# Hybrid decoder layer on one core: gate rows of the second half of the tokens taken from two forms of x that q and k use

## The chip, the core and the metric

One core of a Trainium2 chip runs the whole program. The time is device microseconds of one execution; the median of the runs counts. The engines that matter here are TensorE (PE, with its weight loads PEld), VectorE (DVE), ScalarE (ACT), GpSimd (POOL) and SyncE (SP), which issues most of the DMAs. Each engine takes its instructions in the order in which they stand in its own list and waits on semaphores where an operand or a buffer isn't ready.

## What is computed

One decoder layer on x of 1024 tokens by 1024 channels in float32: rms norm, gated linear attention (GLA), residual; rms norm, a squared-ReLU MLP with 4096 hidden units, residual; final rms norm. What bears on the change is the input projection and the gates:

```python
proj = h @ w_in                          # h = rms_norm(x) * g_mix
q, k, v, r, gk_low = split(proj)         # 512, 512, 1024, 1024 and 16 columns
log_a = log_sigmoid(gk_low @ w_gk_up + b_gk) / 16
b = cumsum(log_a)                        # per chunk; decays are exp(b), exp(-b)
```

q and k are multiplied by decays from `log_a`, and then the tokens go through the attention chunk by chunk.

## The kernel before

**Products.** Each float32 operand is split into a high part (ScalarE, line 81, a copy rounded to fp32r) and a low part (VectorE, line 82, the difference), and a product is three matmuls: high by high, high by low, low by high. A projection is made by a seven-product scheme of 2 by 2 blocks: block names "11", "12", "21", "22" mean half of the channels and half of the tokens (for x) or of the columns (for a weight), and the seven operands are such blocks or sums of them. A step is one of the seven products: 48 matmuls of 512 columns in four lanes (128 rows of output each) and two halves of the channels. Operands of a step are made one step ahead, from tiles `big` (8 buffers, four for a step).

**Order.** q and k together are one projection with steps Q0 to Q6, which take the products in the order 0, 5, 1, 2, 3, 4, 6; then v has V0 to V6, and r has R0 to R4 (two of its products are done later). After that come eight chunks of the attention, the output projection, and the MLP. In the profiled run Q0 begins at 6.5 us, Q1 at 21.4, Q2 at 32.6, Q5 at 65.9, V0 at 87.7, R0 at 169.6, the chunks at 220, the output projection at 299; PE's last matmul ends at 985.6. PE's list is written by hand: it follows the program's text, with functions hung in between by `hooks` (keys are projection, step, and for some a lane and a quarter of the channels). The lists of the other engines are made by a scheduler from the program's priorities and from an `order_after` here and there, which puts one instruction behind another in the list.

**x in forms.** In Q the x blocks come in as `vx` tiles, get scaled by g_mix (line 366 on ScalarE, line 388 on GpSimd) and are combined: step Q1 uses block 21, Q2 uses 12 - 11, Q4 uses 22, and Q5 uses 22 - 12. Each pair of split operands is kept in HBM (`keep`, line 360) for v and r.

**Evacuations.** A product ends in four PSUM banks: tags `gl` (5 banks) and `mm` (3 banks). `qk_into` (from line 475) copies the first product's banks to `hq` on ScalarE (line 485) and adds the later ones on VectorE (line 481).

**Gates.** `wgs` holds w_gk split into high and low parts, laid out so that one 128-column weight load serves both (`split_gate`, line 436, 4 ScalarE and 4 VectorE instructions). The 16 gate columns need 16 matmuls for each half of the tokens ("gate rows", in a bank `mm`). The first half's run between Q0 and Q1 (`gk_first`), from the operands of products 0 and 5, and ScalarE copies them out (line 831). The second half's need blocks 12 and 22 of x: `x12_load` brings block 12 again, `x12_split` scales and splits it in V4, and `gk_second` runs 8 matmuls ahead of V5 and 8 near its end. `token_rms` squares the token rows for the rms; `spread_rms` (line 525) turns four rms columns into a 128 by 512 tile: VectorE writes 8 diagonals (line 534), PE multiplies them by ones (two matmuls), ScalarE copies the bank (line 538), VectorE multiplies the gate rows by it (line 543), and the product is split (lines 544 and 545). `gate_in` multiplies by w_gk_up, and `prep_fast` makes decays per head and multiplies q and k by them (from line 572).

Of the kernel before, what the change touches and what calls it, by code (L numbers as in the profile page):

```python
# [48 lines left out]
def hybrid_trunk(ctx: ExitStack, tc: tile.TileContext, x, xT, w_head, w_r, w_gk, w_up,  # L49
# [10 lines left out]
    def new(tag, dtype=F32):  # L60
        count[0] += 1
        pool_ = ps if tag in ("mm", "gl") else sb
        return pool_.tile(SHAPE.get(tag, [P, 1024]), dtype, tag=tag, bufs=BUFS[tag], name=f"{tag}{count[0]}")

    def f32(ap):
        return ap.bitcast(F32)

    def mm(o, w, m, start, stop, partial=False):

        pe.matmul(o, w, m, start=start, stop=stop, skip_group_check=partial)  # L70
# [50 lines left out]
    def run(general):  # L121
# [312 lines left out]
        wgs5 = wgs.rearrange("p (k g b r) -> p k g b r", k=8, g=4, b=2)  # L434
        wus = new("wup", F32R)

        def split_gate():
# [8 lines left out]

        box = {}

        def gk_rows(pg, kts, part, start, stop):

            for kt in kts:
                for hl in range(2):
                    mm(pg, wgs[:, kt * P:(kt + 1) * P], part(kt, hl), start and kt == kts[0] and hl == 0,
                       stop and kt == kts[-1] and hl == 1)
            return pg

        def token_rms(ts):
            for t in ts:
# [18 lines left out]
        def qk_into(n, lane, p_):  # L477
            d = qk_view(int(PART[n][0]) - 1, lane)[:, half(int(PART[n][1]) - 1)]
            with tc.high_priority():
                if n in (3, 4, 5):  # L480
                    op = dve.tensor_tensor(d, p_, d, op=ALU.add)
                    if n == 5 and lane:
                        order_after(tc, op, last["s1" if lane == 1 else "s1_low"], wait=False)
                else:
                    op = act.activation(d, p_, AF.Copy)
                    if n == 0:
                        order_after(tc, op, last["split"], wait=False)

        v = {}

# [34 lines left out]
        def spread_rms(hf):  # L525

            u, st = new("g4", F32R), new("st", F32R)
            rh, rl, r = st[:, 0:4], st[:, 4:8], rstd1[:, hf * 4:hf * 4 + 4]
            dve.tensor_copy(rh, r)
            dve.tensor_tensor(rl, r, f32(rh), op=ALU.subtract)  # L530
            pb = new("mm")
            for l, part_ in enumerate((rh, rl)):
                for c in range(4):
                    dve.tensor_scalar(u[:, l * 512 + c * P:l * 512 + c * P + P], ident, f32(part_)[:, c:c + 1], None, op0=ALU.mult)
                mm(pb, ones_r, u[:, half(l)], l == 0, l == 1)
            w_ = new("g4")
            dg, rbc = w_[:, 512:1024], w_[:, 0:512]
            act.activation(rbc, pb, AF.Copy)
            if hf == 0:
                box["gk"] = new("g4", F32R)  # L540
            raw, gk = box["raw"][hf], box["gk"][:, half(hf)]
            dst = raw if hf == 0 else dg
            dve.tensor_tensor(dst, raw, rbc, op=ALU.mult)
            act.activation(gk, dst, AF.Copy)
            dve.tensor_tensor(gk[64:128, :], dst[64:128, :], f32(gk[64:128, :]), op=ALU.subtract)


        def chunks(ap):
# [262 lines left out]
        xlive = {}  # L811
        xq_split = xq.split

        xq.first = lambda n, kh: scale_x(kh, *{5: ("21",), 1: ("11", "12"), 2: ("22",)}.get(n, ()))

        def remember(n):
            xlive[n] = xq_split(n)
# [2 lines left out]
        xlive[0] = ops_a[0][1]  # L820

        xk, xr_ = KeptX((0, 5)), KeptX()

        def gk_first():
            pg = gk_rows(new("mm"), range(KT), lambda kt, hl: xlive[0 if kt < 4 else 5][kt % 4 // 2][:, kt % 2, hl, :], True, True)
            box["raw"] = [pg]

        def gk_first_out():
            u, pg = new("g4"), box["raw"][0]
            box["raw"] = [u[:, 0:512]]  # L830
            act.activation(u[:, 0:512], pg, AF.Copy)  # L831

        def x12_load():
            box["x12"] = [new("raw"), new("g4")]
            for kh in range(2):
                nc.sync.dma_start(box["x12"][kh].rearrange("p (k t) -> p k t", k=2), x_piece(2 * kh, 2, 1))

        def x12_split():
            for kh in range(2):
                raw, hi, lo = box["x12"][kh], new("g4", F32R), new("g4" if kh else "raw", F32R)  # L840
                for k in range(2):
                    scaled_split(hi[:, half(k)], lo[:, half(k)], raw[:, half(k)], 2 * kh + k)
                box["x12"][kh] = hi, lo

        def gk_second(part):
            if part == 0:
                box["raw"].append(gk_rows(new("mm"), range(4, KT), lambda kt, hl: xk.tiles[3][kt % 4 // 2][:, kt % 2, hl, :], True, False))
            else:
                gk_rows(box["raw"][1], range(4), lambda kt, hl: box["x12"][kt // 2][hl][:, half(kt % 2)], False, True)

        wv = weight_side(True, from_v, dve, late=True)
        wR = weight_side(True, from_r, dve, late="r")
# [10 lines left out]
        hooks = {(0, 1): (gk_first,), (0, 1, "then"): (gk_first_out,), (0, 3): (split_up,),  # L863
                 (0, 4): (g(token_rms, range(0, 4)),), (0, 5): (g(token_rms, range(4, 8)),),
                 (1, 0, 0, 3): (g(spread_rms, 0),),
                 (2, 4): (r_last,),
                 (1, 2): (x12_load,), (1, 4): (x12_split,), (1, 5): (g(gk_second, 0),),
                 (1, 5, 3, 3): (g(gk_second, 1),), (1, 6, 0, 1): (g(spread_rms, 1),)}
        if not general:
            hooks.update({(1, 0, 2, 3): (g(gate_in, 0, 0, "mm"), g(gate_in, 1, 0, "mm")),  # L870
                          (1, 0, 3, 3): (g(gate_in, 2, 0, "mm"),),
                          (1, 1, 0, 1): (g(gate_in, 3, 0, "mm"), g(prep_fast, 0, 0)),
                          (1, 2): (x12_load,),
                          (1, 2, "then"): (g(prep_fast, 1, 0),), (1, 3, "then"): (g(prep_fast, 2, 0),),
                          (1, 4): (), (1, 4, "then"): (g(prep_fast, 3, 0), x12_split),
                          (1, 5): (g(gk_second, 0),),
                          (1, 6, 3, 1): (g(gate_in, 0, 1, "mm"), g(prep_fast, 0, 1)),
                          (2, 0, 0, 0): (g(gate_in, 1, 1, "mm"), g(prep_fast, 1, 1)),
                          (2, 0, 0, 2): (g(gate_in, 2, 1, "mm"),), (2, 0, 1, 0): (g(gate_in, 3, 1, "mm"),),
                          (2, 0, 3, 3): (g(prep_fast, 2, 1),), (2, 3, "then"): (g(prep_fast, 3, 1),),  # L880
                          (2, 4, 2, 1): (g(operands, 0, "mm"),)})
        chunks_of([(wqk, xq, 0, qk_into, PLAIN), (xk, wv, 1, v_into, PLAIN), (xr_, wR, 1, r_into, R_FIRST)], ops_a, hooks, {},
                  turns={(0, 1): ("X", split_gate, "W"), (0, 2): ("x", "X", "w", "W", lambda: last.update(sums=last["split"], s1=last["sum"], s1_low=last["low"]), "n"),
                         (0, 3): ("W", "x", "X", "n"), (2, 3): ("x", "X", "W", g(wR.sums, 3))})

        last_v = box["v"]
# [7 lines left out]
        if not general:  # L894
            v_split(1)
        for c in range(TT):
            if c == 4 and not general:

                over = new("st")
                dve.tensor_reduce(over[:, 0:1], top, axis=mybir.AxisListType.X, op=ALU.max)  # L900
                dve.tensor_scalar(over[:, 1:2], over[:, 0:1], RANGE, None, op0=ALU.is_gt)
                pf = new("gl")
                mm(pf[:, 0:1], ones, over[:, 1:2], True, True)
                dve.tensor_copy(flag, pf[:, 0:1])
            more = c + 1 < TT
            if general:
                if c % 4 == 0:
                    for h in range(H):
                        prep_general(h, c // 4)
                operands(c)  # L910
                if c:
                    v_split(c)
            elif more:
                operands(c + 1, "mm")
                if c:
                    v_split(c + 1)
            if more:
                if c or general:
                    load_xt(*R_PARTS[c + 1])
                if c in (2, 4):  # L920
                    load_r(5 + c // 2)
            r_part(*R_PARTS[c])
            outputs(c)
            if more:
                new_state(c)
            if c:
                outputs_T(c - 1)
# [312 lines left out]
```

## Time and profile before

| | |
|---|---|
| median of 3 runs | 996.23 us (995.94 to 997.4) |
| profiled execution | 996.73 us, its span 995.0 us |
| granted TensorE clock, mean | 0.997 |
| instructions in the span | 12256 |
| moved by DMA | 193.65 MB, mean 195 GB/s |
| PE waiting for others, whole span | 1.8 us in three waits |
| DMA share of Q3, Q4, Q5, Q6 | 0.84, 0.93, 0.95, 1.05 |

Tile names in the profile leave numbers out: `g` is a tile of tag g4 (gate rows, token rows and others), `mm` and `gl` are PSUM banks, `wa` and `wb` weights, `raw` sums of x. In a row of the timeline stand start, length, engine, line, operation, out<-in, shape, count, and in brackets the idle time before it with what ended it. Line numbers are those of the kernel that the row belongs to.

### The profile page before, as it was taken

Reading aid. Unit: us, or ns where it says so; the run is one execution under the profiler, and the core shown is the slowest. Engines: PE = TensorE matmul, PEld = TensorE weight load, DVE = VectorE, ACT = ScalarE, POOL = GpSimd, SP = SyncE. Lnnn points to the kernel's source line nnn. Section 1 sums busy time; section 2 is a strip of 40 time slices with the busy share of each in tenths; the row PEclk is TensorE's granted clock in tenths of the full one; section 3 lists DMA queues with packets and bytes.
Section 4 is the critical chain, followed back from the end, with each engine's and each line's share of the span. In section 5 each row is a group of like instructions: output and inputs, shape, how many; then the busy total and the mean of one; then the engine's idle time right before and its main releaser. Section 6 shows DMA issues by size and latency. Waiting matters only on the chain.

```text
span 995.0 us, 12256 instructions
## 1 busy us (share of the span) xinstructions
PE 983.5 (99%) x4508; PEld 820.4 (82%) x4508; DVE 748.7 (75%) x912; ACT 564.1 (57%) x860; POOL 237.0 (24%) x146
## 2 busy tenths in 40 slices
PE   9999999999999999999999999999999999999996
PEld 7788888889988888888888888888888888888885
DVE  5996796768899999699662359974339966569976
ACT  7785564887894376666524446332447433566455
POOL 3000010213440000224042142233133224242270
PEclk9999999999999999999999999999999999999998
DMA  9899786575373257651225993367683225971004
GB/s 271 313 319 380 282 295 215 212 242 196 118 280 108 85 196 312 254 221 33 84 99 206 298 303 89 83 175 260 223 324 100 65 63 212 365 283 49 1 1 173
DMA packets 135693, 193.65 MB, mean 195 GB/s; under 512 B 39240, under 2 KB 100808, under 8 KB 124104
## 3 DMA queue, kind: packets, MB, share of 16 engines
q1 hardware_dynamic: 135064, 192.37, 56.0%
q8 instruction: 37, 0.61, 0.3%
q10 hardware_dynamic: 560, 0.40, 0.1%
q14 instruction: 32, 0.26, 0.1%
HBM read 146.62 MB, written 46.14 MB: 194 GB/s over the span
## 4 chain that ended last, share of the span: by engine, by line
PE 92%; DMA 2%; DVE 2%; ACT 2%; SPq 1%; issue 1%; DVEq 0%; ACTq 0%
PE gl L70 61%; PE mm L70 30%; DMA wb<-in_w_head 1%; DMA wa<-in_w_head 1%; DVE vx L1096 0%; PE mm L657 0%; DVE big L82 0%; ACT g L717 0%; PE mm L736 0%; ACT wb L81 0%; SPq L337 0%; DVE big L804 0%; PE gl L736 0%; DVE g L1137 0%; DVE g L726 0%
## 5 line engine op out<-in xcount | busy, mean ns | idle before, releaser
L70 PE MATMUL gl<-big,big 128*128 128x512 f32 x2700 | 626.4, 389 | 0.7 <-DVE big L82 0.4
L70 PEld LDWEIGHTS gl<-big,big 128*128 128x128 f32 x2700 | 506.5, 188 | 106.5 <-DVE big L82 1.1
L70 PE MATMUL mm<-big,big 128*128 128x512 f32 (+1 forms) x1248 | 291.7, 387 | 0.0
L70 PEld LDWEIGHTS mm<-big,big 128*128 128x128 f32 x1248 | 232.7, 188 | 48.2 <-ACT g L831 0.5
L82 DVE TENSOR_TENSOR big<-wa,big 128x1024 fp32r<-128x1024 f32 (+1 forms) x118 | 155.2, 1335 | 85.6 <-ACT big L81 84.6
L81 ACT ACTIVATE big<-wa 128x1024 fp32r<-128x1024 f32 (+1 forms) x118 | 119.2, 1039 | 127.5 <-PE gl L70 67.0
L186 POOL TENSOR_TENSOR wa<-wa,wb 128x1024 f32<-128x1024 f32 x14 | 42.0, 3011 | 299.9 <-DVE big L82 205.9
L186 POOL TENSOR_TENSOR wa<-wa,wa 128x1024 f32<-128x1024 f32 x28 | 80.0, 2866 | 132.8 <-DVE big L82 132.1
L82 DVE TENSOR_TENSOR big<-wb,big 128x1024 fp32r<-128x1024 f32 x50 | 64.4, 1305 | 27.8 <-ACT big L81 27.8
L81 ACT ACTIVATE big<-wb 128x1024 fp32r<-128x1024 f32 x50 | 51.1, 1054 | 56.8 <-PE gl L70 26.6
L82 DVE TENSOR_TENSOR big<-hq,big 128x1024 fp32r<-128x1024 f32 x48 | 61.5, 1290 | 26.7 <-ACT big L81 26.6
L82 DVE TENSOR_TENSOR big<-raw,big 128x1024 fp32r<-128x1024 f32 x42 | 67.6, 1630 | 4.9 <-ACT big L81 4.9
L81 ACT ACTIVATE big<-hq 128x1024 fp32r<-128x1024 f32 x48 | 48.7, 1052 | 39.4 <-PE gl L70 19.5
L81 ACT ACTIVATE big<-raw 128x1024 fp32r<-128x1024 f32 x42 | 43.4, 1055 | 37.9 <-DVE raw L186 17.8
L186 POOL TENSOR_TENSOR wa<-wb,wa 128x1024 f32<-128x1024 f32 x14 | 41.1, 2947 | 39.7 <-DVE big L82 39.7
L577 POOL COPY top<-g 128x4 f32<-128x4 f32 x8 | 10.1, 1267 | 167.8 <-DVE g L569 167.8
L1030 ACT ACTIVATE hq<-hq 128x1024 f32<-128x1024 f32 x24 | 25.3, 1056 | 40.9 <-DVE hq L1023 40.9
L699 POOL TENSOR_SCALAR g<-g,est 128x256 f32<-128x256 f32 x28 | 29.2, 1059 | 52.2 <-DVE g L696 33.3
L1021 ACT ACTIVATE hq<-gl 128x512 f32<-128x512 f32 x36 | 21.4, 593 | 30.6 <-PE gl L70 30.6
L70 PE MATMUL gl<-wb,wa 128*128 128x256 f32 x180 | 32.1, 310 | 0.0
L1023 DVE TENSOR_TENSOR hq<-gl,hq 128x512 f32<-128x512 f32 x24 | 16.0, 685 | 19.8 <-PE gl L70 19.8
L1068 DVE TENSOR_TENSOR vx<-gl,vx 128x512 f32<-128x512 f32 x44 | 29.1, 679 | 0.9 <-PE gl L70 0.8
(206 smaller groups left out, 898.7 us busy)
## 6 DMA issues: line engine op xcount, KB each, us to landing
big<-xw SPq DMA_DIRECT2D x42, 1024.0 KB, 6.9
big<-xv SPq DMA_DIRECT2D x20, 1024.0 KB, 6.4
xv<-big SPq DMA_DIRECT2D x14, 1024.0 KB, 8.5
xw<-big SPq DMA_DIRECT2D x14, 1024.0 KB, 4.3
wa<-in_w_ff SPq DMA_DIRECT2D x32, 256.0 KB, 4.0
wb<-in_w_ff SPq DMA_DIRECT2D x32, 256.0 KB, 3.9
wa<-in_w_ff SPq DMA_DIRECT2D x16, 512.0 KB, 6.6
wb<-in_w_ff SPq DMA_DIRECT2D x16, 512.0 KB, 5.5
```

The lines of the kernel that those rows point to most:

```text
L70: pe.matmul(o, w, m, start=start, stop=stop, skip_group_check=partial)
L81: last["split"] = act.activation(hi, src, AF.Copy)
L82: last["low"] = dve.tensor_tensor(lo, src, f32(hi), op=ALU.subtract)
L186: op = self.eng.tensor_tensor(*(self.ap(b, kp, 2) for b in (o, x_, y_)), op=op)
L577: pool.tensor_copy(top[:, 8 * h + 4 * hf:8 * h + 4 * hf + 4].unsqueeze(2), a[:, :, P - 1:P])
L699: pool.tensor_scalar(S[:, vs], Z[:, vs], g, None, op0=ALU.mult)
L1021: act.activation(d, p_, AF.Copy)
L1023: dve.tensor_tensor(d, p_, d, op=ALU.add)
L1030: act.activation(d2, d2, AF.Relu)
L1068: dve.tensor_tensor(yd, p_, yd, op=ALU.add)
```

## The change

The second half's gate rows are taken from the operands of Q4 (22) and Q5 (22 - 12). Since x12 W1 + x22 W2 = x22 (W1 + W2) - (x22 - x12) W1, new gate weights W1 + W2 and -W1 are formed and split (`split_gate_again`), and the 16 matmuls run between Q4 and Q5. The loading, scaling and splitting of block 12 in V goes. `spread_rms(1)` moves from V6 to V0, one lane behind `spread_rms(0)`; the first heads' decays move about one step up, and those of the second half from V6 to R3 into V5 to R0. ScalarE's first four evacuations (product 0) are put behind the scalings and splits of Q2's x, and the copy of the first gate bank goes in between the scalings. The range check's two VectorE instructions move from chunk 4 to chunk 2. The diff, cut:

```diff
+        def split_gate_again():
+            t = wgu[:, 128:256]
+            for op in (dve.tensor_tensor(t[:, 0:64], wgr[:, 0:64], wgr[:, 64:128], op=ALU.add),
+                       dve.tensor_scalar(t[:, 64:128], wgr[:, 0:64], -1.0, None, op0=ALU.mult)):
+                order_after(tc, op, last["low"], wait=False)
+            box["wgs"] = new("g4", F32R)
+            split_gate(box["wgs"], t.rearrange("p (k r) -> p k r", r=16))
...
+        def gk_rows(wgs, forms):
+
+            box["pg"] = new("mm")
+            for kt in range(KT):
                 for hl in range(2):
+                    mm(box["pg"], wgs[:, kt * P:(kt + 1) * P], forms[kt // 4][kt % 4 // 2][:, kt % 2, hl, :],
+                       kt + hl == 0, kt + hl == KT)
+
+        def gk_out(hf):
+            if hf == 0:
+                box["raw"] = new("g4")
+            act.activation(box["raw"][:, half(hf)], box["pg"], AF.Copy)
...
+                elif n == 0:
+                    box.setdefault("q0", []).append((d, p_))
                 else:
-                    op = act.activation(d, p_, AF.Copy)
-                    if n == 0:
-                        order_after(tc, op, last["split"], wait=False)
+                    act.activation(d, p_, AF.Copy)
+
+        def qk_first_out():
+            for d, p_ in box["q0"]:
+                order_after(tc, act.activation(d, p_, AF.Copy), last["split"], wait=False)
...
+        def x_first(n, kh):
+            if (n, kh) == (1, 1):
+                gk_out(0)
+            scale_x(kh, *{5: ("21",), 1: ("11", "12"), 2: ("22",)}.get(n, ()))
+        xq.first = x_first
...
-        def gk_first():
-        def gk_first_out():
-        def x12_load():
-        def x12_split():
-        def gk_second(part):
...
+        hooks = {(0, 1): (lambda: gk_rows(wgs, (xlive[0], xlive[5])),),(0, 3): (split_up,), (0, 4, "then"): (split_gate_again,),
+                 (0, 4): (g(token_rms, range(0, 4)),), (0, 5): (g(token_rms, range(4, 8)), lambda: gk_rows(box["wgs"], (xlive[3], xlive[4]))),
+                 (0, 5, "then"): (g(gk_out, 1),),
+                 (1, 0, 0, 3): (g(spread_rms, 0),), (1, 0, 1, 3): (g(spread_rms, 1),),
...
-            if c == 4 and not general:
+            if c == 2 and not general:
 
                 over = new("st")
```

Three places in the engines' lists show what moves. ScalarE (ACT) between Q0 and Q2, before: vx_170 and vx_171 are the two halves of x's block 12, hq the evacuations of product 0, mm_286 the first gate bank, big_315 and big_318 the x operands of Q2.

```order
L81 ACTIVATE big_225<-wb_163 128x2x512
L485 ACTIVATE hq_271<-gl_228 128x512
L485 ACTIVATE hq_271<-gl_232 128x512
L485 ACTIVATE hq_280<-gl_240 128x512
L485 ACTIVATE hq_280<-gl_236 128x512
L366 ACTIVATE vx_170<-vx_170,vec 128x512 x2
L366 ACTIVATE vx_171<-vx_171,vec 128x512 x2
L831 ACTIVATE g_335<-mm_286 128x512
L81 ACTIVATE big_315<-raw_307 128x2x512
L81 ACTIVATE big_318<-raw_308 128x2x512
```

The same place in the changed kernel, where the gate bank is mm_282 and the operands of Q2 are big_313 and big_316:

```order
L81 ACTIVATE big_225<-wb_163 128x2x512
L366 ACTIVATE vx_170<-vx_170,vec 128x512 x2
L366 ACTIVATE vx_171<-vx_171,vec 128x512
L470 ACTIVATE g_306<-mm_282 128x512
L366 ACTIVATE vx_171<-vx_171,vec 128x512
L81 ACTIVATE big_313<-raw_303 128x2x512
L81 ACTIVATE big_316<-raw_304 128x2x512
L506 ACTIVATE hq_271<-gl_228 128x512
L506 ACTIVATE hq_271<-gl_232 128x512
L506 ACTIVATE hq_278<-gl_236 128x512
L506 ACTIVATE hq_278<-gl_240 128x512
```

The evacuations now stand behind the splits of Q2's x, and the gate bank's copy stands in front of all of them. On VectorE the two sums of weights for Q2 (wa) also stand together now, ahead of the first two adds from Q1's banks.

VectorE around the end of Q4, before: gl_415, mm_422, mm_429 and mm_436 are Q4's four lanes, big_564 and big_567 the x operand of Q5, big_660 a weight of Q6.

```order
L186 TENSOR_TENSOR vx_171<-vx_191,vx_171 128x1024
L481 TENSOR_TENSOR hq_271<-gl_415,hq_271 128x512
L82 TENSOR_TENSOR big_564<-vx_170,big_564 128x2x512
L481 TENSOR_TENSOR hq_271<-mm_422,hq_271 128x512
L481 TENSOR_TENSOR hq_280<-mm_429,hq_280 128x512
L82 TENSOR_TENSOR big_567<-vx_171,big_567 128x2x512
L481 TENSOR_TENSOR hq_280<-mm_436,hq_280 128x512
L82 TENSOR_TENSOR big_660<-wb_174,big_660 128x2x512
```

The same place now; g_155 holds the gate weights as loaded and their new sums, g_574 their high and low parts, which PE reads in the 16 matmuls between Q4 and Q5, and big_688 and big_691 are weights of Q6:

```order
L186 TENSOR_TENSOR vx_171<-vx_191,vx_171 128x1024
L82 TENSOR_TENSOR big_564<-vx_170,big_564 128x2x512
L496 TENSOR_TENSOR hq_271<-gl_415,hq_271 128x512
L496 TENSOR_TENSOR hq_271<-mm_422,hq_271 128x512
L82 TENSOR_TENSOR big_567<-vx_171,big_567 128x2x512
L496 TENSOR_TENSOR hq_278<-mm_429,hq_278 128x512
L445 TENSOR_TENSOR g_155<-g_155 128x64
L446 TENSOR_SCALAR g_155<-g_155 128x64
L82 TENSOR_TENSOR big_688<-wb_174,big_688 128x2x512
L496 TENSOR_TENSOR hq_278<-mm_436,hq_278 128x512
L82 TENSOR_TENSOR g_574<-g_155,g_574 128x8x16 x4
L82 TENSOR_TENSOR big_691<-wb_175,big_691 128x2x512
```

The four low parts of g_574 stand behind the add of Q4's last lane and behind the low part of big_688. On ScalarE their high parts stand behind that of big_691, whose buffer held a weight of Q4 until that step's end.

VectorE around V0, before: g_839 are the diagonals of the first spreading, g_854 its copy, g_335 the gate rows, g_856 their split, big_806 to big_817 the operands of V1.

```order
L534 TENSOR_SCALAR g_839<-ident,st_840 128x128 x8
L530 TENSOR_TENSOR st_1383<-rstd_86,st_1383 128x4
L82 TENSOR_TENSOR big_806<-vx_158,big_806 128x2x512
L82 TENSOR_TENSOR big_807<-vx_159,big_807 128x2x512
L82 TENSOR_TENSOR big_814<-wb_654,big_814 128x2x512
L82 TENSOR_TENSOR big_817<-wb_655,big_817 128x2x512
L186 TENSOR_TENSOR wa_820<-wa_728,wb_734 128x1024
L186 TENSOR_TENSOR wa_821<-wa_729,wb_735 128x1024
L543 TENSOR_TENSOR g_335<-g_335,g_854 128x512
L545 TENSOR_TENSOR g_856<-g_335,g_856 64x512
```

The same place now, from the operands of V1 on; g_904 are the diagonals of the second spreading, which PE multiplies right after V0's second lane:

```order
L82 TENSOR_TENSOR big_836<-vx_159,big_836 128x2x512
L186 TENSOR_TENSOR wa_850<-wa_758,wb_764 128x1024
L82 TENSOR_TENSOR big_843<-wb_682,big_843 128x2x512
L82 TENSOR_TENSOR big_846<-wb_683,big_846 128x2x512
L560 TENSOR_TENSOR g_306<-g_306,g_883 128x512
L553 TENSOR_SCALAR g_904<-ident,st_905 128x128 x4
L562 TENSOR_TENSOR g_885<-g_306,g_885 64x512
L553 TENSOR_SCALAR g_904<-ident,st_905 128x128 x4
L560 TENSOR_TENSOR g_306<-g_306,g_919 128x512
L562 TENSOR_TENSOR g_885<-g_306,g_885 64x512
```

The second spreading's diagonals stand behind the first spreading's product (L560), four of them behind its split (L562) as well.

More of the change, by code (lines that the diff above doesn't have):

```diff
@@ L535, in spread_rms @@
                 mm(pb, ones_r, u[:, half(l)], l == 0, l == 1)
-            w_ = new("g4")
-            dg, rbc = w_[:, 512:1024], w_[:, 0:512]
+            rbc = new("g4")[:, 0:512]
             act.activation(rbc, pb, AF.Copy)
@@ L540, in spread_rms @@
                 box["gk"] = new("g4", F32R)
[L541 to L545, printed above, removed]
+            raw, gk = box["raw"][:, half(hf)], box["gk"][:, half(hf)]
+            dve.tensor_tensor(raw, raw, rbc, op=ALU.mult)
+            act.activation(gk, raw, AF.Copy)
+            dve.tensor_tensor(gk[64:128, :], raw[64:128, :], f32(gk[64:128, :]), op=ALU.subtract)
         def chunks(ap):
@@ L862, in run @@
         fine_steps.add((0, 0))
[L863 to L868, printed above, removed]
+        hooks = {(0, 1): (lambda: gk_rows(wgs, (xlive[0], xlive[5])),),(0, 3): (split_up,), (0, 4, "then"): (split_gate_again,),
+                 (0, 4): (g(token_rms, range(0, 4)),), (0, 5): (g(token_rms, range(4, 8)), lambda: gk_rows(box["wgs"], (xlive[3], xlive[4]))),
+                 (0, 5, "then"): (g(gk_out, 1),),
+                 (1, 0, 0, 3): (g(spread_rms, 0),), (1, 0, 1, 3): (g(spread_rms, 1),),
+                 (2, 4): (r_last,)}
@@ L876, in run @@
[L876 to L880, printed above, removed]
+                          (1, 0, 3, 3): (g(gate_in, 2, 0, "mm"), g(prep_fast, 0, 0)),
@@ new lines, in run @@
+                          (1, 1, 0, 1): (g(gate_in, 3, 0, "mm"), g(prep_fast, 1, 0)),
+                          (1, 2, "then"): (g(prep_fast, 2, 0),), (1, 3, "then"): (g(prep_fast, 3, 0),),
+                          (1, 5, 0, 3): (g(gate_in, 0, 1, "mm"), g(gate_in, 1, 1, "mm")), (1, 5, 2, 3): (g(prep_fast, 0, 1),),
+                          (1, 6, 0, 1): (g(gate_in, 2, 1, "mm"), g(gate_in, 3, 1, "mm")), (1, 6, 3, 1): (g(prep_fast, 1, 1),),
+                          (2, 0, 0, 0): (g(prep_fast, 2, 1),), (2, 0, 3, 3): (g(prep_fast, 3, 1),),
@@ L881, in run @@
                           (2, 4, 2, 1): (g(operands, 0, "mm"),)})
         chunks_of([(wqk, xq, 0, qk_into, PLAIN), (xk, wv, 1, v_into, PLAIN), (xr_, wR, 1, r_into, R_FIRST)], ops_a, hooks, {},
-                  turns={(0, 1): ("X", split_gate, "W"), (0, 2): ("x", "X", "w", "W", lambda: last.update(sums=last["split"], s1=last["sum"], s1_low=last["low"]), "n"),
+                  turns={(0, 1): ("X", g(split_gate, wgs, wgr3), "W"), (0, 2): ("x", "X", qk_first_out, "w", "W", lambda: last.update(sums=last["split"], s1=last["sum"], s1_low=last["low"]), "n"),
@@ L901, in run @@
                 dve.tensor_scalar(over[:, 1:2], over[:, 0:1], RANGE, None, op0=ALU.is_gt)
+            if c == 4 and not general:
                 pf = new("gl")
```

32 lines of the change are left out of this document (2 added, 30 removed).

## The prediction

> **What bounds the kernel now.** I read the page first, then who PE waited for, then the instructions of PE, ScalarE (ACT) and VectorE (DVE) in order of time around each place that the change touches, and last the table by stages. The page's first part and the view of waits (engine, line, who was waited for: total, times, longest):
>
> ```profile
> PE 983.5 (99%) x4508; PEld 820.4 (82%) x4508; DVE 748.7 (75%) x912; ACT 564.1 (57%) x860; POOL 237.0 (24%) x146
> ...
> ...
> PE gl L70 <- DVE big L82: 0.4, 1, 0.4
> PE gl L70 <- ACT big L81: 0.3, 1, 0.3
> ```
>
> TensorE sets the time, and it waits for hardly anything. A busy PE need not be at its peak, so I check the rate in the timeline (start, length, instruction, count). Q1 ends and Q2 starts at 32.64, and Q4 ends and Q5 starts at 65.93:
>
> ```profile
> 22.75 4.58 PE L70 MATMUL mm<-big,big 128*128 128x512 f32 x18
> 27.18 1.55 PE L70 MATMUL gl<-big,big 128*128 128x512 f32 x6
> ...
> 32.64 0.61 PE L70 MATMUL gl<-big,big 128*128 128x512 f32 x2
> 33.61 1.19 PE L70 MATMUL gl<-big,big 128*128 128x512 f32 x4 [0.35 <-DVE big L82]
> ...
> 65.93 24.64 PE L70 MATMUL gl<-big,big 128*128 128x512 f32 x108
> 90.41 0.62 PE L70 MATMUL mm<-g,ones_r 128*128 128x512 f32 x2
> ```
>
> From 65.93 to 90.41 are 108 matmuls: 0.2267 us each, a step of 48 is 10.88 us, a lane's half (6) 1.36. By the same rate 22.75 + 18 x 0.2267 = 26.83, so 0.35 us are lost before 27.18, and 32.64 + 0.45 = 33.09, so 0.52 before 33.61. The view of waits has no further one in Q, V and R. So of everything the change does there, at most 0.87 us can be won; anything that arrives late is lost in full, since nothing behind it has slack.
>
> **Term 1, the first evacuations on ScalarE.** The two gaps have these releasers (weight loads, ScalarE, VectorE, and the chain of waits):
>
> ```profile
> 25.66 1.24 PEld L70 LDWEIGHTS mm<-big,big 128*128 128x128 f32 x6 [0.45 <-ACT g L831]
> ...
> 20.65 2.04 ACT L485 ACTIVATE hq<-gl 128x512 f32<-128x512 f32 x4
> 22.56 2.57 ACT L366 ACTIVATE vx<-vx,vec 128x512 f32<-128x512 f32 x4
> 25.01 0.60 ACT L831 ACTIVATE g<-mm 128x512 f32<-128x512 f32 x1
> ...
> 28.87 1.22 DVE L186 TENSOR_TENSOR wa<-wa,wb 128x1024 f32<-128x1024 f32 x1
> 30.01 0.68 DVE L481 TENSOR_TENSOR hq<-gl,hq 128x512 f32<-128x512 f32 x1
> 30.61 1.21 DVE L186 TENSOR_TENSOR wa<-wa,wb 128x1024 f32<-128x1024 f32 x1
> ...
> 32.34 2.35 DVE L82 TENSOR_TENSOR big<-wa,big 128x1024 fp32r<-128x1024 f32 x2
> ...
> 24.77 4.65 DMA wa<-in_w_head
> ```
>
> Before, PE waits for the copy of the gate bank (25.01 to 25.61), queued behind four evacuations and four scalings. Behind those evacuations the scalings start 1.91 us sooner (20.65 instead of 22.56); three of them, 0.61 each, and the copy end near 23.1, ahead of 25.5 when PE wants the bank. The 0.35 goes. What is late next is Q2's weight sum. VectorE's sums of x wait for these scalings and so start some 1.4 us sooner, and its first weight sum is done before the second half of the weights lands, at 24.77 + 4.65 = 29.42. From there: second sum 1.14, two adds of 0.60, low part 1.22: 29.42 + 1.14 + 1.20 + 1.22 = 32.98, and PE at 33.03 instead of 33.61. Value -0.58; bounds 0 (x lands late, and VectorE is no further on than before) and -0.87 (both gaps). VectorE and PE both gain this 0.58, so distances between them in Q3 and Q4 stay as they are; the times below are those of before.
>
> **Term 2, the second gate rows between Q4 and Q5.** PE's 16 matmuls (3.63 us) are only moved: the same number went away in V5. But they start where Q5 started, T = 65.93, and need all four high and low parts of the new gate weights. The rows that the new order is filled with:
>
> ```profile
> 60.05 2.35 DVE L186 TENSOR_TENSOR vx<-vx,vx 128x1024 f32<-128x1024 f32 x2
> 62.32 0.68 DVE L481 TENSOR_TENSOR hq<-gl,hq 128x512 f32<-128x512 f32 x1
> 62.92 1.21 DVE L82 TENSOR_TENSOR big<-vx,big 128x1024 fp32r<-128x1024 f32 x1
> 64.06 1.41 DVE L481 TENSOR_TENSOR hq<-mm,hq 128x512 f32<-128x512 f32 x2
> 65.38 1.22 DVE L82 TENSOR_TENSOR big<-vx,big 128x1024 fp32r<-128x1024 f32 x1
> ...
> 13.08 0.88 DVE L82 TENSOR_TENSOR g<-g,g 128x128 fp32r<-128x128 f32 x4
> 12.26 0.90 ACT L81 ACTIVATE g<-g 128x128 fp32r<-128x128 f32 x4
> 77.01 2.01 ACT L81 ACTIVATE big<-wa 128x1024 fp32r<-128x1024 f32 x2 [3.37 <-PE gl L70]
> ...
> 55.05:65.90 10.85, 10.85 (x49) 9.01 (x48) 10.81 (x12) 7.72 (x12) 0.00 (x0) 1.00 0.93 360
> ```
>
> In the last row (stage, PE, PEld, DVE, ACT busy) VectorE is busy 10.81 of 10.85 us: it has no room in Q4. Its new order (names as in the rows of the section before), each instruction 1.14 (1024 wide) or 0.60 to 0.66 (512 wide) behind the last: the low part of big_564 from 62.37 (behind the sums of 60.05), two adds from 63.5, the low part of big_567 from 64.7, an add from 65.85, the two small gate sums from 66.45 (64 wide; taken as 0.13 each, under the 0.21 of 128-wide ones, 1.65 / 8 in Term 3), the low part of big_688 from 66.7, an add from 67.85, and from 68.45 the gate weights' four low parts, 4 x 0.22 = 0.88: 69.35. PE stands from 65.93 to 69.4: +3.4. ScalarE gives the other bound: its high parts are queued behind that of big_691, whose buffer is read to the end of Q4; a row like it (77.01) starts 0.2 us after PE's step ended at 76.81, so 66.13 + 0.95 + 0.90 + a last low part 0.27 = 68.25, or +2.3. Nothing in the order can be quicker than that. I take 3.4, because VectorE's rows are the later. Behind the waiting matmul stand all of Q5 and everything after it.
>
> **Term 3, the second spreading of rms in V0.** It stood in V6, 70 us after its inputs; now PE wants it one lane after the first spreading, and half of its diagonals stand behind VectorE's work on the first. S is V0's start, 87.69 = 65.93 + 2 x 10.88:
>
> ```profile
> 91.20 0.59 ACT L538 ACTIVATE g<-mm 128x512 f32<-128x512 f32 x1
> 94.74 0.63 ACT L544 ACTIVATE g<-g 128x512 fp32r<-128x512 f32 x1 [0.23 <-DVE g L543]
> ...
> 80.91 1.65 DVE L534 TENSOR_SCALAR g<-ident,st 128x128 fp32r<-128x128 f32 x8
> 89.47 2.36 DVE L82 TENSOR_TENSOR big<-wb,big 128x1024 fp32r<-128x1024 f32 x2 [3.56 <-ACT big L81]
> 94.02 0.68 DVE L543 TENSOR_TENSOR g<-g,g 128x512 f32<-128x512 f32 x1
> 95.41 0.69 DVE L545 TENSOR_TENSOR g<-g,g 64x512 fp32r<-64x512 f32 x1 [0.70 <-ACT g L544]
> ```
>
> The low parts end at 91.83, ScalarE's copy of the first spreading at 91.79, both S + 4.1. Then VectorE: product 0.61, four diagonals 0.82, the gate's low part 0.61 (ScalarE's split, 0.63, is done by then), four diagonals 0.82: S + 7.0. PE asks for the second half after 24 matmuls of two lanes, two of the first spreading and one of the second: 27 x 0.2267 = S + 6.1. Term: +0.9; bounds +0.5 and +1.3, four handovers between engines being worth 0.1 each way.
>
> **At nothing.** The second x block is no longer loaded, scaled and split (two loads of 512 KB; four ScalarE and four VectorE instructions of 512): they lay in V4, where PE never waited. The gates' decays come one step sooner, into V0 and V1; the row below shows 6.8 us of idle VectorE there, against 3.4 per head (four scans 1.36, three operations near 0.68). If that cover failed, a head's 3.4 would show. The loads of the last four tokens are now behind the kept forms of x on SP, and the last of them must wait for the old gate weights; even with the 11.1 us of the slowest group its square comes before Q6 needs sums that stand behind it on VectorE, with about 1 us to spare; beyond that, each us late costs one. The range check's two small instructions move two chunks up: 0, plus or minus 0.2.
>
> ```profile
> 102.89 0.75 DVE L500 SCALAR_TENSOR_TENSOR vx<-gl,tok,vx 128x512 f32<-128x512 f32 x1 [6.80 <-PE gl L70]
> 113.06 1.36 DVE L569 TENSOR_TENSOR_SCAN g<-g 128x128 f32<-128x128 f32 x4
> ...
> g<-in_x SPq DMA_DIRECT2D x3, 512.0 KB, 11.1
> ```
>
> **Sum.** -0.58 + 3.4 + 0.9 = +3.7 us. The profiled execution took 996.73 (span 995.0), 0.5 above the median of 996.23; so 1000.4 for it and 999.9 for the median.
>
> **Rivals.**
> *The wait is covered.* If VectorE is 3.4 us further on at Q4's end than I count, the gate weights are ready at T, and -0.58 + 0.9 are left: 996.5, no slower. It decides at one point, the end of the fourth low part against T. For it: ScalarE has 3 us of room in Q4 and could make the parts soon. Against it: VectorE's 10.81 of 10.85.
> *ScalarE sets the wait, not VectorE.* Terms at their low ends: -0.58 + 2.3 + 0.5 = +2.2, 998.4. Against it: the low parts are VectorE's, and stand behind two 1024-wide and four 512-wide operations.
> *The clock falls in the new wait.* These rows show the granted clock at the end (last but two numbers; PE's last matmul ends at 985.6) and PE's start and a later run of the same width:
>
> ```profile
> 985.00:990.00 5.00, 0.62 (x6) 0.41 (x4) 3.02 (x10) 2.92 (x10) 0.00 (x0) 0.97 0.63 229
> 990.00:995.00 5.00, 0.00 (x0) 0.00 (x0) 0.00 (x0) 0.00 (x0) 0.00 (x0) 0.50 0.30 103
> ...
> 1.10 5.06 PE L70 MATMUL gl<-ones 128*128 128x128 f32 x22 [1.10 <-DVE ones L90]
> 220.75 0.89 PE mm L70 x8
> ```
>
> A mean of 0.97 puts the fall to 0.50 at 989.7, 4.1 us after PE stopped. PE's first 22 matmuls took 0.23 us each against 0.11 later, so 5 us ran at half rate. If the new wait reached such a fall, 5 us at half rate would cost 2.5 more: 1002.4. Against it: 3.4 is under 4.1. The Trainium skill ("TensorE: Matmul & The Clock Gate", Part 1) speaks against the change here: one whole idle window of about 3.4 us, running freely, halves the clock. By that rule a wait of 3.4 us falls only if it meets a window exactly; the trace's 4.1 agrees with it.
> *It gets faster.* All of Term 1's 0.87 and over 1.1 us of the small gaps of the chunk stage, which the change doesn't touch: under 994.2.
>
> **How the numbers follow.** Runs of this kernel differ by 1.5 us, so 0.2% (2.0 us) is about what can be told from no change. My forecast has 0.62, ScalarE's bound 0.13, the clock 0.08, covered 0.14, faster 0.03. Covered and faster (0.17) are left out below the range, which runs from 997.8 (ScalarE's bound less 0.6) to 1002.4. Slower by over 0.2% means over 998.2: nearly all of the forecast and the clock, half of ScalarE's case: 0.76. Same: 0.21.
>
> **What would show it.** Right: PE idle before the matmuls of the second gate rows, some 3 us, released by VectorE's line 82 on a g tile; near 1 us before the second spreading's second matmul; no wait on the gate bank's copy near 25, and PE restarting near 33.0. The granted clock stays 1.00. Wrong: the second gate rows following Q4 without a gap, or a wait in V or R on decays that came too soon.

## The result and the profile after

The changed kernel takes 1002.76 us (median of 5 runs, 1002.39 to 1004.65) against 996.23 us for the kernel before (5 runs, 995.70 to 997.40): ratio 1.0068, interval 1.0053 to 1.0083. It is slower, and a little above the upper end of the predicted range. The profiled execution took 1003.06 us, its span is 1001.2 us. Its mean granted clock is 0.995, as in all five runs; in the kernel before it was 0.997.

The view of waits of the changed kernel (who waited, for whom: total, times, longest):

```profile
PE mm L70 <- DVE g L82: 3.3, 1, 3.3
...
PE mm L70 <- DVE g L553: 1.0, 1, 1.0
PE gl L70 <- DVE big L82: 0.7, 1, 0.7
```

Two are new: the parts of the second gate weights (line 82 on a `g` tile) and the diagonals of the second spreading (line 553). TensorE's timeline around them, with Q1 and Q2's start first and its last product at the end:

```profile
22.41 4.24 PE L70 MATMUL mm<-big,big 128*128 128x512 f32 x18
...
31.93 0.61 PE L70 MATMUL gl<-big,big 128*128 128x512 f32 x2
33.23 1.21 PE L70 MATMUL gl<-big,big 128*128 128x512 f32 x4 [0.69 <-DVE big L82]
...
61.51 4.24 PE L70 MATMUL mm<-big,big 128*128 128x512 f32 x18
69.04 5.53 PE L70 MATMUL mm<-big,g 128*128 128x512 f32 x16 [3.29 <-DVE g L82]
74.41 24.64 PE L70 MATMUL gl<-big,big 128*128 128x512 f32 x108
...
102.09 0.40 PE L70 MATMUL mm<-g,ones_r 128*128 128x512 f32 x1
103.44 0.50 PE L70 MATMUL mm<-g,ones_r 128*128 128x512 f32 x1 [0.95 <-DVE g L553]
...
988.48 1.72 PE L70 MATMUL mm<-big,big 128*128 128x256 f32 x13
```

Reckoned from start to start at 0.2267 us a matmul, Q4 ends at 61.51 + 18 x 0.2267 = 65.59, 0.34 sooner than before (65.93). These 0.34 us are not the change's: the 18 matmuls of Q1 that start at 22.75 before already start at 22.41 now. Q0 itself starts at 5.98 instead of 6.48, when its first weights have landed (ScalarE splits them from 5.30 instead of 5.80), and what stands ahead of Q0 is the same in both kernels. From these 18 matmuls to Q4's end both kernels take 43.18 us. TensorE then stands until 69.04: 3.45 us. The 16 gate matmuls should take 3.63, but Q5 starts at 74.41, 5.37 later: 1.74 us are lost while TensorE is at work. The second spreading costs 103.44 - 102.09 - 0.23 = 1.12. Together -0.34 + 3.45 + 1.74 + 1.12 = +5.97; TensorE's last product starts at 988.48 instead of 982.59, +5.89. In sum less than 0.1 us is lost or won in the 885 us between.

The 1.74 us are in the table by stages. Its windows here are cut at the points where the granted clock changes (columns: stage, length, then busy time of PE, PEld, DVE, ACT, POOL with the number of instructions; the last but two is the granted clock):

```profile
66.79:70.20 3.41, 1.16 (x5) 0.98 (x6) 3.33 (x7) 0.91 (x5) 0.00 (x0) 1.00 0.96 289
70.20:73.61 3.41, 3.41 (x10) 2.66 (x9) 1.84 (x2) 2.12 (x2) 0.00 (x0) 0.50 1.00 408
73.61:995.21 921.60, 916.69 (x4218) 764.98 (x4217) 688.99 (x844) 513.72 (x787) 227.82 (x131) 1.00 0.53 183
```

TensorE is at work in all of 70.20 to 73.61, but at half speed: 3.41 / 2 = 1.71 us. Behind it the clock stays up to 995.21, past TensorE's last matmul. The stage before the slow one, as long, holds 1.16 us of work and 2.25 us of idling, yet not one idle stretch of 3.41.

### The profile page after: what moved, and what is told of

It reads as the page before. It is cut to its first block, busy times and chain, and to the rows that moved or that the text cites. A ratio compares the mean times of both kernels' runs of the same rounds, so it can differ in the third digit from the quotient of the medians.

```text
span 1001.2 us, 12257 instructions
## 1 busy us (share of the span) xinstructions
PE 984.9 (98%) x4508; PEld 821.0 (82%) x4508; DVE 750.2 (75%) x914; ACT 564.4 (56%) x861; POOL 236.7 (24%) x146
## 4 chain that ended last, share of the span: by engine, by line
PE 90%; DVE 5%; ACT 2%; issue 1%; DMA 0%; SPq 0%; DVEq 0%; ACTq 0%
PE gl L70 60%; PE mm L70 29%; DVE big L82 2%; DVE wa L186 0%; ACT big L81 0%; DVE vx L1086 0%; DVE hq L496 0%; PE mm L674 0%; DMA wa<-in_w_head 0%; DVE raw L186 0%; ACT g L734 0%; PE mm L753 0%; ACT wb L81 0%; DVE big L821 0%; PE gl L753 0%
## 5 line engine op out<-in xcount | busy, mean ns | idle before, releaser
L82 DVE TENSOR_TENSOR big<-raw,big 128x1024 fp32r<-128x1024 f32 x42 | 67.7, 1629 | 6.4 <-ACT big L81 6.0
```

Of the source, the lines that this page charges most:

```text
L82: last["low"] = dve.tensor_tensor(lo, src, f32(hi), op=ALU.subtract)
```

## What was tested

**Theory.** The granted clock is judged in fixed windows of 3.41 us; a window that is idle for a good part, though not for all of it, halves the clock for the next. The new wait between Q4 and Q5 therefore costs 3.45 by itself and some 1.7 more behind it; the spreading costs 1.12. **Rivals.** The 1.74 us belong to the gate matmuls (their operands, their bank) and not to idling; or an idle stretch must itself be 3.4 us long. The first four experiments were laid out before the table above was read as fixed windows.

### 12 matmuls in the wait

Matmuls from Q4's operands into the gate bank, which is written over afterwards, fill the wait. The weights come no sooner, and the results of the 12 are used by nothing.

```diff
             box["pg"] = new("mm")
+            if wgs is not first_wgs:
+                x = xlive[3][0]
+                for _ in range(12):
+                    mm(box["pg"], x[:, 0, 0, 0:P], x[:, 0, 0, :], True, True)
             for kt in range(KT):
```

> The changed kernel, with 12 more matmuls of 512 columns between Q4 and the second gate rows; they write into the gate bank, which the first gate matmul then overwrites, so the result is the same. They take 12 x 0.2267 = 2.7 us out of a wait of 3.45. Theory (the idle wait lowers the granted clock, and the half rate after it costs 1.7 us): VectorE's end of the gate weights stays where it is, PE's idle time falls to about 0.7 us, the clock stays at 1.00, the 16 gate matmuls take 3.6 us and not 5.4, and the time falls by 1.7 to about 1001.0. Rival (the 16 matmuls are slow for their own sake, through late operands or shared reads, and the clock shown is another thing): they stay at 5.4 us and the time stays at 1002.8.

Measured: 1000.92 us (1000.77 to 1002.54), ratio 1.0044 (1.0030 to 1.0058), mean clock 0.997. Its timeline of TensorE:

```profile
65.74 2.88 PE L70 MATMUL mm<-big 128*128 128x512 f32 x12
69.23 3.92 PE L70 MATMUL mm<-big,g 128*128 128x512 f32 x16 [0.61 <-DVE g L82]
73.00 24.64 PE L70 MATMUL gl<-big,big 128*128 128x512 f32 x108
```

The gate matmuls start at much the same time after Q4 (3.49 us instead of 3.45) with the same operands, and take 3.77 instead of 5.37. The median is 1.84 us lower with 12 matmuls more (2.45 lower by its distance to the kernel before, which took 996.84 beside it). The rival that puts the loss on the gate matmuls falls: it was the idling ahead of them.

### The weights one step sooner

```diff
-(0, 4, "then"): (split_gate_again,)
+(0, 3, "then"): (split_gate_again,)
```

> The changed kernel, with the new gate weights formed and split one step sooner (behind the operands of Q4 and not of Q5). Theory (PE waits 3.45 us for them, and the half clock follows from that wait): no wait between Q4 and Q5, clock 1.00 throughout, 5.2 us less: about 997.6. VectorE's 1.1 us of work for them then lie in Q3 or Q4, where Q5's operands have some 5 us of room, so nothing else is late. Rival (VectorE has no room in Q2 to Q4, and the 1.1 us come back as a wait for operands or banks): a new wait of about 1 us at Q4, Q5 or Q6, about 998.7. Rival (the loss lies in the moved decays of V and R): 1001 or more.

Measured: 1002.33 us (1000.51 to 1003.31), ratio 1.0049. A miss. The wait between Q4 and Q5 is gone, as expected; two others took its place in V0. TensorE's timeline there:

```profile
94.29 2.90 PE L70 MATMUL gl<-big,big 128*128 128x512 f32 x12
98.96 0.51 PE L70 MATMUL mm<-g,ones_r 128*128 128x512 f32 x1 [1.77 <-DVE g L553]
100.57 0.50 PE L70 MATMUL mm<-g,ones_r 128*128 128x512 f32 x1 [1.10 <-DVE g L553]
100.91 4.51 PE L70 MATMUL gl<-big,big 128*128 128x512 f32 x12
105.26 0.63 PE L70 MATMUL mm<-g,wup 128*128 128x512 f32 x2
```

VectorE's timeline, and the table by stages behind it:

```profile
92.89 2.36 DVE L82 TENSOR_TENSOR big<-wb,big 128x1024 fp32r<-128x1024 f32 x2 [2.99 <-ACT big L81]
95.16 2.35 DVE L186 TENSOR_TENSOR wa<-wa,wb 128x1024 f32<-128x1024 f32 x2
97.44 0.68 DVE L560 TENSOR_TENSOR g<-g,g 128x512 f32<-128x512 f32 x1
98.04 0.87 DVE L553 TENSOR_SCALAR g<-ident,st 128x128 fp32r<-128x128 f32 x4
98.94 0.69 DVE L562 TENSOR_TENSOR g<-g,g 64x512 fp32r<-64x512 f32 x1
99.64 0.87 DVE L553 TENSOR_SCALAR g<-ident,st 128x128 fp32r<-128x128 f32 x4
```

```profile
98.13:101.54 3.41, 1.48 (x5) 1.03 (x6) 2.34 (x9) 1.06 (x2) 0.00 (x0) 1.00 0.37 154
101.54:104.95 3.41, 3.41 (x9) 2.64 (x9) 1.38 (x2) 0.79 (x2) 0.00 (x0) 0.50 0.00 0
```

Moving one hook made the scheduler order VectorE's list in V0 anew: both sums of weights (95.16, 2.35 us) now stand between the low parts and the gate's product, where the changed kernel has both ahead of the low parts and the product right behind them. Reckoned from Q5's start, the product and the diagonals come 2.2 us later for it. The spreading loses 1.95 + 1.38 us (start to start, less 0.227 a matmul), and the clock falls behind it: 12 matmuls take 4.35 instead of 2.72, 1.63 more. That is the same mechanism at another place, with the idling in two pieces (98.13 to 98.96, and about 99.47 to 100.57). Of the five runs two had a mean clock of 0.997, and these were at 1000.51 and 1000.80; the three at 0.993 to 0.994 were at 1002.33 to 1003.31.

### The second spreading at the end of V1, and both moves together

```diff
-(1, 0, 1, 3): (g(spread_rms, 1),)
+(1, 1, 3, 3): (g(spread_rms, 1),)
```

> The changed kernel, with the second spreading of rms at the end of V1 and not behind the second lane of V0. Theory (PE waits 1.1 us for its diagonals, since four of them stand behind the first spreading's split on VectorE): that wait goes, nothing else changes, about 1001.7. Rival (the time at that place is lost to VectorE's load in V0 whatever PE asks for first): the wait moves to the matmuls of the gates behind it, 1002.8.

> The changed kernel with both edits, early gate weights and late second spreading. Theory (three losses of 3.45, 1.74 and 1.1 and a gain of 0.35 at Q2 are all there is): about 996.2 - 0.35 = 995.9, the kernel before within what can be told. Rival (decays that come too soon, or the order of loads, cost something in V and R): over 997.

Measured: 1010.10 us (4 runs, 1009.74 to 1010.94), ratio 1.0134, for the first; 1006.72 us (1005.40 to 1009.78), ratio 1.0104, for both moves together. Both miss. TensorE and VectorE at the spreading, in the first of them:

```profile
112.49 8.32 PE L70 MATMUL mm<-big,big 128*128 128x512 f32 x36
125.78 1.58 PE L70 MATMUL mm<-g,ones_r 128*128 128x512 f32 x2 [4.97 <-DVE g L553]
127.16 2.76 PE L70 MATMUL gl<-big,big 128*128 128x512 f32 x6
```

```profile
123.00 1.36 DVE L586 TENSOR_TENSOR_SCAN g<-g 128x128 f32<-128x128 f32 x4
124.28 0.26 DVE L553 TENSOR_SCALAR g<-ident,st 128x128 fp32r<-128x128 f32 x1
124.45 0.69 DVE L595 TENSOR_TENSOR g<-g 128x512 f32<-128x512 f32 x1
125.06 1.46 DVE L553 TENSOR_SCALAR g<-ident,st 128x128 fp32r<-128x128 f32 x7
```

The diagonals went behind a scan of the decays on VectorE (and part of them behind the next operation on those, line 595), and came 5.1 us too late instead of 1.1. A later hook is no later deadline for VectorE alone: it moves the instructions down its list too. Behind the wait two windows ran at half clock. In this profile TensorE also restarted in Q2 1.3 us later (34.54), some 70 us ahead of what the edit moves: VectorE's second sum of weights starts at 30.93 instead of 29.62, after 1.64 us of waiting for a load. Why that load came later stays open. In the version with both moves the spreading waits 5.72 us, and there too two windows at half clock follow.

### 4 and 8 matmuls in the wait

The edit of the first experiment, with 4 and with 8. This asks how much idling the clock bears.

> The changed kernel with 4 instead of 12 matmuls, written over later, between Q4 and the second gate rows: the wait for the weights' low parts keeps its end (69.04), but TensorE idles for 3.45 - 4 x 0.227 = 2.54 us of it instead of 3.45. Theory W (the clock is judged in fixed windows of 3.41 us, and one that is idle for a good part, between 1.13 and 1.90 us by the windows before the falls seen so far, halves the clock for the next): the clock falls still wherever 1.9 us or more of the 2.54 lie in one window: about 1002.7 and a mean clock of 0.995. Rival L (only an idle stretch of 3.4 us or more does it): no fall, about 1001.0 and 0.997.

> The same with 8 matmuls: TensorE idles for 3.45 - 8 x 0.227 = 1.64 us. It lies between the 1.13 us that did not halve the clock and the 1.90 us that did. Theory W with its bound above 1.64: no fall, about 1001.0, clock 0.997; with its bound below: a fall where all of it lies in one window, up to 1002.7, clock 0.995. Rival L: no fall, 1001.0.

Measured, with 4: 1002.72 us (1001.36 to 1003.16), ratio 1.0060 (1.0046 to 1.0074); the mean clock is 0.995 in three runs (1002.72 to 1003.16), 0.996 in one (1001.86) and 0.997 in one (1001.36). With 8: 1000.66 us (1000.00 to 1001.63), ratio 1.0040 (1.0027 to 1.0054), and 0.997 in all five. The profiled execution with 4 was the one without a fall, though it idles 2.6 us ahead of the gate matmuls. The table by stages, cut in steps of 3.413 us counted back from where its clock falls behind the last matmul (992.49):

```profile
67.48:70.89 3.41, 1.69 (x7) 1.43 (x8) 2.80 (x7) 0.79 (x3) 0.00 (x0) 1.00 0.98 296
70.89:74.30 3.41, 3.41 (x16) 2.81 (x15) 2.36 (x2) 2.69 (x4) 0.00 (x0) 1.00 1.03 422
```

The idling lies across the border at 67.48, so the emptier of the two windows still holds 1.69 us of work. By the times and mean clocks, then, an idle stretch of 2.5 to 2.6 us, far under 3.4, does halve the clock in most runs and not in every one, while one of 1.6 to 1.7 us did in none of five. The rival that wants a stretch of 3.4 us falls. That the same program falls in one run and not in the next fits windows that are fixed on the chip and not on the program.

### The second spreading 12 matmuls later in V0

```diff
-(1, 0, 1, 3): (g(spread_rms, 1),)
-(1, 0, 2, 3): (g(gate_in, 0, 0, "mm"), g(gate_in, 1, 0, "mm")),
+(1, 0, 2, 3): (g(gate_in, 0, 0, "mm"), g(gate_in, 1, 0, "mm"), g(spread_rms, 1)),
```

> The changed kernel with the second spreading 12 matmuls later in V0, behind the first two gate inputs, instead of among V1's steps: TensorE gets there at about 105.5 us, VectorE's eight rows are done at about 104.0. Theory (the rows are only some 1.1 us late, and a wait goes that is given 2.7 us more of matmuls): the wait of 1.12 us goes and nothing takes its place, 1002.76 - 1.12 = about 1001.6, clock 0.995 as after. Rival (whatever moves the spreading puts it behind the gates' steps on VectorE, as at V1's end): a wait of 1 to 5 us stays, 1002.7 to 1008.

Measured: 1001.58 us (999.17 to 1003.59), ratio 1.0044 (1.0030 to 1.0057). The spreading's wait is gone and nothing took its place. The wait of 3.49 us between Q4 and Q5 is still there, and the five runs show what it is worth by itself: 999.17 at a mean clock of 0.997; 1001.12, 1001.58 and 1002.44 at 0.995 to 0.996; and the profiled 1003.59 at 0.994. In that one the clock is down for two windows:

```profile
65.28:68.69 3.41, 1.22 (x6) 0.68 (x4) 3.41 (x6) 1.85 (x5) 0.00 (x0) 1.00 0.99 413
68.69:72.10 3.41, 2.27 (x5) 1.82 (x6) 2.22 (x6) 0.16 (x1) 0.00 (x0) 0.50 1.01 311
72.10:75.52 3.42, 3.42 (x9) 2.63 (x8) 2.01 (x2) 1.96 (x2) 0.00 (x0) 0.50 1.03 414
```

The idling from 66.34 to 69.83 lies across the border at 68.69: 2.35 us in one window, 1.14 in the next. Matmuls run at half rate for 2.27 + 3.42 us, half of which is lost: 2.8. The fastest run is 4.4 us under this one, the slowest, with the same program; these 2.8 are part of it, if the fastest had no fall, as its mean clock says. Another 0.7 were lost ahead of Q1, which starts at 21.77 here and at 21.05 in the changed kernel's trace.

### Both waits taken away

The weights one step sooner as above, and the second spreading behind the third gate input:

```diff
-(0, 4, "then"): (split_gate_again,)
+(0, 3, "then"): (split_gate_again,)
...
-(1, 0, 1, 3): (g(spread_rms, 1),)
-(1, 0, 3, 3): (g(gate_in, 2, 0, "mm"), g(prep_fast, 0, 0)),
+(1, 0, 3, 3): (g(gate_in, 2, 0, "mm"), g(spread_rms, 1), g(prep_fast, 0, 0)),
```

> The changed kernel with the new weights made one chunk step sooner and the second spreading 18 matmuls later in V0, behind the first three gate inputs. Theory: the version with the sooner weights alone lost 1.95 + 1.38 us at the second spreading and 1.63 us to a half clock behind it, and nothing else; VectorE's rows are there at about 101.1 us, TensorE comes at about 102.9, so all 4.96 us go: 1002.33 - 4.96 = about 997.4, clock 0.997. Rival (the waits move on to the gates' inputs and decays behind it): 999 to 1002.

Measured: 997.36 us (11 runs, 996.42 to 998.96) against 996.73 us for the kernel before on the same chip, ratio 1.0007 (0.9998 to 1.0016): not to be told from the kernel before, and 5.4 us under the changed one. TensorE's timeline has neither wait:

```profile
61.91 4.24 PE L70 MATMUL mm<-big,big 128*128 128x512 f32 x18
65.99 3.89 PE L70 MATMUL mm<-big,g 128*128 128x512 f32 x16
...
103.53 0.62 PE L70 MATMUL mm<-g,ones_r 128*128 128x512 f32 x2
```

The two waits and the half clock behind them are the whole loss, within that interval (-0.2 to +1.6 us). What the decays that come sooner and the loads that the change drops cost or bring is no more than that.

### ScalarE's part alone

The kernel before, with Q0's copies and the first gate rows' copy behind x's scalings and nothing else (`gk_first_out` is called in `x_first`, `qk_first_out` in the turns of Q2, both as in the change):

```diff
-                 (0, 1, "then"): (gk_first_out,),
...
-(0, 2): ("x", "X", "w", "W",
+(0, 2): ("x", "X", qk_first_out, "w", "W",
```

> The kernel before with the ScalarE part of the change alone: Q0's copies and the first gate rows' copy behind x's scalings. Theory (term 1 by its measured size): the 0.35 us at the gate bank's copy go, Q2 restarts as its data lands, and Q4 ends about 0.35 sooner: before's median less 0.35, about 996.4, clock 0.997; the gap ahead of Q2's second product stays between 0.5 and 0.9 us. Rival (the copies, now later, hold TensorE's banks or VectorE's sums up): a new wait of up to 1 us in Q1 or Q2 and before's median plus 0 to 0.7.

Measured: 996.32 us (11 runs, 995.45 to 996.96) against 996.59 us, ratio 0.9999 (0.9990 to 1.0008): a gain of 0.3 us lies within that interval, and so does none. In its profiled execution the gaps in Q1 and at Q2 are gone: TensorE runs into Q2 at 31.80 and on without a gap, where one of 0.5 to 0.9 us was expected to stay. This execution is the fastest of the eleven, and its Q0 too starts 0.55 us sooner (5.93). Its timeline, and in the second view the second sum of weights on VectorE:

```profile
27.72 4.24 PE L70 MATMUL mm<-big,big 128*128 128x512 f32 x18
31.80 1.52 PE L70 MATMUL gl<-big,big 128*128 128x512 f32 x6
```

```profile
28.31 1.23 DVE L186 TENSOR_TENSOR wa<-wa,wb 128x1024 f32<-128x1024 f32 x1 [0.51 <-DMA vx<-in_xT]
```

## Why the prediction was wrong

**Term 1**, -0.58 predicted, nothing measured. The wait on the gate bank goes, as worked out: the copy stands among the scalings, far ahead of 25.5, and the gap in Q1 is gone in all ten traces with this edit. But in the changed kernel's trace the gap at Q2 takes its place: it grows from 0.52 to 0.85 us (31.93 + 0.45 to 33.23). VectorE's second sum of weights starts at 29.62, and not at 29.42 less the 0.34 us that the program was ahead; it waits for a load. That is the term's bound of 0, where what is needed next lands late. The 0.34 us by which Q4 ends sooner come from Q0's start, ahead of everything that the change touches, and are luck; the expectations above that count them as this term's gain (0.35) misread them too. ScalarE's and VectorE's timelines of the changed kernel:

```profile
22.37 0.58 ACT L470 ACTIVATE g<-mm 128x512 f32<-128x512 f32 x1
...
65.85 1.06 ACT L81 ACTIVATE big<-wb 128x1024 fp32r<-128x1024 f32 x1 [1.79 <-PE mm L70]
66.81 0.89 ACT L81 ACTIVATE g<-g 128x128 fp32r<-128x128 f32 x4
```

```profile
29.62 1.23 DVE L186 TENSOR_TENSOR wa<-wa,wb 128x1024 f32<-128x1024 f32 x1 [0.50 <-DMA vx<-in_xT]
...
66.37 1.22 DVE L82 TENSOR_TENSOR big<-wb,big 128x1024 fp32r<-128x1024 f32 x1
67.50 0.68 DVE L496 TENSOR_TENSOR hq<-mm,hq 128x512 f32<-128x512 f32 x1
68.10 0.88 DVE L82 TENSOR_TENSOR g<-g,g 128x128 fp32r<-128x128 f32 x4
```

That sum starts at 28.31 in the run with ScalarE's part alone, and there both gaps go. In the ten traces with this edit it starts at 28.31 to 30.93, and from Q1's 18 matmuls to Q4's end they take 42.16 to 44.25 us, 43.18 in the middle, as the kernel before does. What the term is worth in one execution hangs on when a load lands.

**Term 2**, +3.4 predicted, 3.45 measured, by the steps named: the four low parts (68.10) behind the add of Q4's last lane (67.50) and the low part of a weight of Q6 (66.37). Each stands 0.34 sooner than worked out, as Q4's end does. ScalarE's high parts end near 67.7, ahead of VectorE: the rival that made them set the wait falls, as does the one that had the wait covered.

**Term 3**, +0.9 predicted, 1.12 measured, within its bounds, with half of the diagonals on either side of the gate's low part as expected. No wait on anything that was put at nothing shows in the profile.

**The step that failed** is the dismissal of the rival "the clock falls in the new wait", with its reason "3.4 is under 4.1": the forecast kept the granted clock at 1.00 through the wait, and it fell to 0.50 for one window, which costs 1.74 us. It fell in the profiled run of the changed kernel, and by their mean clock of 0.995 in the other four too. The 4.1 us were read at the end of the program, from TensorE's last matmul at 985.6 to the fall at 989.7. With windows of 3.41 us that row says something else: 985.6 to 986.3 is the rest of a window that was mostly busy, and 986.3 to 989.7 the window that was judged. The stretch from the stop to the fall is not the idling that a fall needs. I took one instance as a threshold, and read the rule of the Trainium skill beside it ("TensorE: Matmul & The Clock Gate", Part 1: a free-running window of about 3.4 us, half clock after an idle one) as asking for a window that is idle from end to end. The window free of the program agrees with the runs here; the whole window idle doesn't: 2.25 us idle and 1.16 busy were enough. The price was off as well, in the other direction: 2.5 us (5 us at half rate) against 1.74 measured, one window of 3.41 at half rate. With that 1.74 the forecast of 999.9 is 1001.6, and with the 0.58 of Term 1 that did not come, 0.05 more for Term 2 and 0.22 more for Term 3 it is 1002.5; the median is 0.3 above that, less than runs of one kernel differ by. The upper end of the range, 1002.4, held that rival with everything else at its forecast value, so with a price 0.76 lower, 0.85 us of terms that came out worse were just enough to go over it. Beside the clock, Term 1 is the step that failed: the load that VectorE waits for took back what ScalarE had gained.

## What to carry to other kernels

A stall on TensorE has two prices: its length, and the half clock that can follow; here a wait of 3.45 us cost 5.2, so price every new wait of 2 us and more with one window at half rate. An operand that a moved product needs must be placed in the lists of the engines that make it, not only ahead in the program's text: after every move compare those lists again, since moving one hook rearranged VectorE's list 25 us later. And read the mean clock of each run beside its time: runs of one program differed by the number of windows that ran at half clock. It is a rough sign only: the half clock behind the last matmul is in it too (989.72 to 995.0 in the kernel before), and one run of that kernel shows 0.946 at an ordinary 995.97 us.

## What the runs showed of the hardware

**The windows.** In every trace with a fall inside the program the half clock lasted 3.41 us or twice that. In the changed kernel it then stayed up for 921.60 us (the last row of its table by stages), which is 270 x 3.413, and in all eleven traces the changes of the granted clock lie whole multiples of 3.413 us apart: the windows run through the program in one fixed raster. Work in a window that was followed by half clock: 1.16 us (changed kernel), 1.22 (spreading later in V0), 1.48 (weights sooner), and 1.51 in the kernel with the spreading in V1, which shows the nearest pair of rows:

```profile
65.06:68.47 3.41, 1.96 (x9) 1.31 (x7) 3.41 (x7) 1.67 (x4) 0.00 (x0) 1.00 1.00 406
68.47:71.88 3.41, 1.51 (x7) 1.25 (x8) 2.98 (x7) 0.78 (x4) 0.00 (x0) 1.00 0.97 298
71.88:75.29 3.41, 3.41 (x10) 2.63 (x9) 2.45 (x2) 1.84 (x2) 0.00 (x0) 0.50 1.02 416
```

1.96 us of work in 3.41 kept the clock up, 1.51 did not. The profile with 4 matmuls in the wait narrows it: 1.69 us (67.48 to 70.89) kept the clock up. The border lies between 44% and 50% of a window by these; the rows are of one core and one kind of matmul, and the exact rule stays open.

**At half clock** a window with 2.27 us of work (68.69 to 72.10 above) didn't bring the clock back, though 1.69 us at full clock had been enough to keep it; a window that was full did. Work counted in clock cycles would explain both, and was not tested.

**The phase.** In the profiled executions the windows' borders lie at different places of the program: 70.20 in the changed kernel, 68.69 with the spreading later in V0. So the same wait, 3.49 us in the profile, was followed by two windows at half clock in one run of that program, and by its mean clocks by one and by none in others.
